# A Strassen layer kernel: loads and rotations in written order, the rotary table by another queue, S4 in S2's place, and another order at the start

## The chip, the cores and the metric

The kernel runs on one core of one Trainium2 chip. The metric is device time in microseconds (us) of one execution; three executions of the kernel before took 1544.78, 1542.77 and 1547.8, median 1544.78. The engines are TensorE (PE, with its weight loads PEld), VectorE (DVE), ScalarE (ACT), GpSimd (POOL) and SyncE (SP, which here only issues DMAs). ACT and POOL issue DMAs too.

## What is computed

One encoder layer for 1024 tokens of width 2048, in float32:

```python
def hybrid_layer(x, w_in, w_out, norm_w, decay_fwd, decay_bwd, gn_w, gn_b, sink):
    h = rms_norm(x, norm_w)
    proj = h @ w_in
    ...
    rq, rk, rv, rg, aq, ak, av, ag = jnp.split(proj, splits, axis=-1)
    y_ret = retention_branch(rq, rk, rv, decay_fwd, decay_bwd, gn_w, gn_b) * jax.nn.silu(rg.astype(jnp.float32))
    y_att = window_attention_branch(aq, ak, av, sink) * jax.nn.silu(ag.astype(jnp.float32))
    y = jnp.concatenate([y_ret, y_att], axis=-1).astype(x.dtype)
    return x + y @ w_out
```

proj has 6656 columns: eight retention heads of 128 (q, k, v and gate), and window attention with eight query heads and two key/value heads. The q and k of both are turned by rotary tables; the retention's covers all 128 columns of a head. A group norm with gn_w and gn_b follows the retention. A final RMSNorm follows the layer.

## The kernel before

**Products.** Both projections are done by Strassen's scheme in Winograd's form: a matrix product of 2 x 2 blocks in seven products, with sums of blocks ahead and behind. For the input projection the inner dimension is cut in two parts, the columns in blocks of 512. A *unit* is one part of one block: its weights are the four quarters a11, a12, a21, a22 (128 x 1024 each, 512 KB), and there are 26 units, in four phases (PHASES). The seven products come in the order 1, 2, 6, 5, 7, 3, 4 and take as weights, in this order, a11, a12, S2 = a22 - S1 (tile s2), S3 = a21 + a22 (kept in a21), S1 = a11 - a21 (kept in a11), S4 = a12 - S2 (kept in a12) and a22. The trace calls all quarters "a" and s2 "s". The x side of the products lies in the tiles c.

Each operand is split for float32 precision: wH is the value rounded by ACT (L87), wL what is left, by DVE (L84). A step is three matmuls of 128 x 512 (mm3): wH by the high part of c (L98), wH by its low part (L99), wL by the high part (L100); a product has 24 matmuls. wH and wL have two buffers, so that operands are made about a product ahead of PE. The results leave PSUM by ACT copies and DVE additions into tiles ct (L259, L91), and from there to DRAM as pr (on SP for the first part, on POOL with addition for the second).

**What sets the order.** PE's, SP's and POOL's instructions stand in the order of the program. advance(), called every six matmuls (a *tick*), lets the running jobs take a step each: attention, retention, gating, loads; idle(n) in a job skips n ticks. ACT's and DVE's instructions are put in written order up to tick 33; from there a scheduler chooses their order. operands() writes the operands of a unit; then(n, k) issues the next unit's quarter on SP at the point where the tile comes free.

**The start.** PE warms up on the identity (L1001), turns vec (norm_w, gn_w and gn_b, 32 rows) to columns (L1008), and transposes x's first four row tiles (xt, L1015). ACT rounds the transposed banks into c (L896), DVE makes the low part (L897, from_bank), and the value itself is kept in src (L902 on ACT, L904 on DVE: keep_bank). The squares of x (L362 on ACT, L364 on DVE) give the RMS factors; the rows of tiles 4 to 7 are scaled by them (scale_x, L377) before their transposes (L383).

**Attention and retention.** rotate() turns the attention's q and k (its products are L482). The softmax of window attention is L560 to L575; it reads the tiles snk and bnd. The retention's heads are fed by next_of(), which loads a head's q or k (tile qT or kT, L689) and its halves swapped (rx, L695) from pr, and multiplies them by the table rot (1 MB, loaded at L863) on DVE (L702, L704). Its decay factors come from decays(). sd are the score tiles of a head.

**The end.** gating() loads mix and pr on ACT's queue, out_operands() and project() run the output projection in four more units, and finish() (from L1308) writes the rows scaled by the final norm's weight fw.

## Time and profile before

| quantity | value |
|---|---|
| median of three executions | 1544.78 us (1542.77 to 1547.8) |
| the profiled execution | 1540.42 us |
| its span, first to last instruction | 1538.6 us |
| mean granted clock of PE | 0.996 |
| PE busy, share of the span | 1515.1 us, 98% |
| DVE busy | 1085.5 us, 71% |
| ACT busy | 688.4 us, 45% |
| POOL busy | 150.8 us, 10% |
| HBM traffic over the span | 204 GB/s |

A row of the timeline has the start in us, the time in us, the engine (SPq is SP's DMA issue), the line of the kernel, the operation, what it writes and reads, and in brackets the idle time of the engine before it with what ended it. A busy share is an average over stages with different limits, so the table by stretches of time is to be read beside it: the busy time of each engine in a stretch, in us, with the number of its instructions.

### The profile page before, as it was taken

What the parts mean: (1) busy time and instruction counts of PE and PEld (TensorE: products, weight loads), DVE (VectorE), ACT (ScalarE), POOL (GpSimd) and SP (SyncE); (2) the same over time, 40 slices, a digit from 0 to 9 for tenths busy, and PEclk for the clock granted to TensorE, in tenths of its full rate; (3) what the DMA queues carried; (4) which work ended last, traced back from release to release, by engine and by line L of the source; (5) the groups of instructions that cost most, each with busy time, mean ns of one, the idle gap of its engine ahead of it and who ended that gap; (6) DMA issues with size and microseconds to landing.
All of it is one profiled execution on the core that took longest, in us unless ns stands there. A gap on an engine that the chain in (4) does not pass through costs nothing.

```text
span 1538.6 us, 20487 instructions
## 1 busy us (share of the span) xinstructions
PE 1515.1 (98%) x7413; PEld 1274.3 (83%) x7413; DVE 1085.5 (71%) x1941; ACT 688.4 (45%) x1147; POOL 150.8 (10%) x168
## 2 busy tenths in 40 slices
PE   8999999999999999998999999999999999999997
PEld 7788888788888888887888888888888888888886
DVE  6885595557757585745877787779756966776766
ACT  6643463234535453533354434444444643543425
POOL 0000001111010000001211100001121102020001
PEclk9999999999999999999999999999999999999999
DMA  8268656899664415787577556469789688394756
GB/s 301 83 219 295 249 189 169 214 229 243 162 193 136 147 61 176 248 285 181 138 184 212 151 192 216 154 236 339 192 251 241 145 278 166 82 205 161 220 178 249
DMA packets 150533, 306.59 MB, mean 199 GB/s; under 512 B 13440, under 2 KB 71200, under 8 KB 141472
## 3 DMA queue, kind: packets, MB, share of 16 engines
q1 hardware_dynamic: 125744, 251.78, 48.0%
q0 software_dynamic: 19584, 35.66, 15.4%
q10 hardware_dynamic: 5104, 17.84, 3.2%
q8 instruction: 58, 0.95, 0.2%
q14 instruction: 43, 0.35, 0.1%
HBM read 190.68 MB, written 122.95 MB: 204 GB/s over the span
## 4 chain that ended last, share of the span: by engine, by line
PE 85%; DMA 6%; DVE 5%; ACT 1%; issue 1%; SPq 1%; POOL 0%; POOLq 0%; DVEq 0%; ACTq 0%
PE pj L100 21%; PE pj L98 21%; PE pj L99 21%; PE ax L99 5%; PE ax L100 5%; PE ax L98 5%; PE ax L771 2%; PE ax L498 1%; DVE wL L84 1%; DMA a<-in_w_in_dram 1%; PE ax L575 1%; DVE c L84 1%; DMA kept<-c 1%; PE ax L818 1%; PE ax L738 1%
## 5 line engine op out<-in xcount | busy, mean ns | idle before, releaser
L98 PE MATMUL pj<-c,wH 128*128 128x512 f32 x1448 | 579.4, 400 | 1.7 <-ACT wH L87 1.7
L100 PE MATMUL pj<-c,wL 128*128 128x512 f32 x1448 | 567.2, 392 | 4.3 <-DVE wL L84 4.1
L99 PE MATMUL pj<-c,wH 128*128 128x512 f32 x1448 | 565.9, 391 | 2.2 <-DVE c L897 1.1
L84 DVE TENSOR_TENSOR wL<-a,wH 128x1024 fp32r<-128x1024 f32 (+1 forms) x185 | 224.8, 1215 | 180.3 <-ACT wH L87 177.6
L100 PEld LDWEIGHTS pj<-c,wL 128*128 128x128 f32 x1448 | 272.3, 188 | 65.2 <-DVE wL L84 7.0
L87 ACT CAST wH<-a 128x1024 fp32r<-128x1024 f32 (+1 forms) x185 | 193.8, 1047 | 282.8 <-PE pj L99 119.6
L99 PEld LDWEIGHTS pj<-c,wH 128*128 128x128 f32 x1448 | 272.9, 188 | 53.7 <-DVE c L84 2.2
L98 PEld LDWEIGHTS pj<-c,wH 128*128 128x128 f32 x1448 | 272.9, 188 | 52.4 <-ACT wH L87 2.2
L259 ACT COPY ct<-pj 128x512 f32<-128x512 f32 x200 | 115.8, 584 | 214.3 <-PE pj L100 213.6
L249 POOL DMA_DIRECT2D pr<-ct x104 | 92.0, 955 | 836.8 <-DVE ct L91 725.0
L91 DVE TENSOR_TENSOR ct<-pj,ct 128x512 f32<-128x512 f32 x170 | 113.6, 687 | 81.2 <-PE pj L100 80.6
L99 PE MATMUL pj<-wL,c 128*128 128x512 f32 x224 | 87.3, 390 | 0.0
L98 PE MATMUL pj<-wH,c 128*128 128x512 f32 x224 | 87.2, 389 | 0.0
L100 PE MATMUL pj<-wH,c 128*128 128x512 f32 x224 | 87.1, 389 | 0.0
L99 PE MATMUL ax<-wL,c 128*128 128x512 f32 x208 | 81.0, 390 | 0.0
L98 PE MATMUL ax<-wH,c 128*128 128x512 f32 x208 | 80.9, 389 | 0.0
L100 PE MATMUL ax<-wH,c 128*128 128x512 f32 x208 | 80.9, 389 | 0.0
L84 DVE TENSOR_TENSOR wL<-s,wH 128x1024 fp32r<-128x1024 f32 x31 | 37.8, 1221 | 27.0 <-ACT wH L87 27.0
L99 PEld LDWEIGHTS pj<-wL,c 128*128 128x128 f32 x224 | 42.0, 188 | 9.1 <-DVE wL L84 0.3
L87 ACT CAST sH<-st 128x128 fp32r<-128x128 f32 x112 | 30.1, 297 | 43.5 <-DVE st L785 29.4
L98 PEld LDWEIGHTS pj<-wH,c 128*128 128x128 f32 x224 | 42.0, 188 | 8.8
L100 PEld LDWEIGHTS pj<-wH,c 128*128 128x128 f32 x224 | 42.0, 188 | 8.6
(222 smaller groups left out, 2023.6 us busy)
## 6 DMA issues: line engine op xcount, KB each, us to landing
a<-in_w_in_dram SPq DMA_DIRECT2D x103, 512.0 KB, 4.8
kept<-c SPq DMA_DIRECT2D x28, 1024.0 KB, 7.6
c<-kept SPq DMA_DIRECT2D x28, 1024.0 KB, 8.9
pr<-ct SPq DMA_DIRECT2D x104, 256.0 KB, 4.9
pr<-ct POOLq DMA_DIRECT2D x104, 256.0 KB, 6.0
a<-in_w_out_dram SPq DMA_DIRECT2D x18, 512.0 KB, 4.7
rx<-pr SPq DMA_DIRECT2D x64, 128.0 KB, 4.9
ysrc<-mix ACTq DMA_DIRECT2D x16, 512.0 KB, 4.9
```

The source lines that it names most:

```text
L84: nc.vector.tensor_tensor(out=dst, in0=src, in1=high.bitcast(F32), op=ALU.subtract)
L87: nc.scalar.copy(out=dst_h, in_=src)
L91: nc.vector.tensor_tensor(out=dst, in0=a, in1=b, op=ALU.add)
L98: nc.tensor.matmul(po, aH, bH, start=first, stop=False, **kw)
L99: nc.tensor.matmul(po, aH, bL, start=False, stop=False, **kw)
L100: nc.tensor.matmul(po, aL, bH, start=False, stop=last, **kw)
L249: nc.gpsimd.dma_start(out=dst, in_=t, accum_op=ALU.add)
L259: nc.scalar.copy(out=t, in_=bank)
L498: nc.tensor.transpose(pt[:, blk(t)], src[:, blk(b * 4 + t)], ident)
L575: nc.tensor.transpose(pt[:, blk(j)], s[:, blk(j)], ident)
L738: nc.tensor.matmul(sc[:, blk(t)], kT[:, c], qT[:, c], start=True, stop=True)
L771: nc.tensor.matmul(p, k_tok[:, c], vd[:, c, d], start=True, stop=True)
```

## The change

The change has several parts that lie at different places of the program.

- **Written order.** behind() keeps an instruction behind all that was written ahead of it for its engine, where the scheduler had a choice. It is used for S1 = a11 - a21 from tick 33 on, for rotate()'s products, for the rotation of the retention's head 0, and for gating's loads.
- **S4 in S2's place.** S4 is written to s2 instead of a12. a12 comes free with its own product's operand, and the next unit's a12 is issued right behind its a11.
- **rot** is issued by POOL at the start of heads() instead of by SP; q's loads of head 0 come four ticks earlier, their swapped halves go to tiles of the tag sd, and the rotation waits four ticks more.
- **The start.** vec is norm_w alone and is issued first on ACT's queue; its transpose stands behind those of x's tile 0. gn_w and gn_b are loaded in decays() and transposed there.
- **x's squares and scaling** come in another order: from_bank is cut into rounded (ACT) and left_over (DVE), and for odd k ACT's second reading of the bank stands ahead of DVE's. x's tiles 6 and 7 are scaled one and two ticks earlier, tile 5 one later, and tile 7 on ACT.
- gating waits six ticks instead of four between loads, and the factor sqrt(D) on fw is taken into the squares (scale D**-0.5) and the constants of the last norm.

```diff
     def sub(dst, a, b):
-        nc.vector.tensor_tensor(out=dst, in0=a, in1=b, op=ALU.subtract)
+        return nc.vector.tensor_tensor(out=dst, in0=a, in1=b, op=ALU.subtract)
...
+    def behind(it, ins):
+
+        if it:
+            tc.keep_in_program_order(ins)
...
             yield operand(a11)
-            yield operand(a12)
+            op = operand(a12)
             s2 = wp.tile([P, M, 2 * P], F32, name="s2", tag="s2")
-            sub(a11, a11, a21)
+            behind(clock[0] >= 33, sub(a11, a11, a21))
             sub(s2, a22, a11)
+            yield op
             yield operand(s2)
             add(a21, a21, a22)
             op = operand(a21)
             then(2, 1)
             yield op
             op = operand(a11)
+            sub(s2, a12, s2)
             then(1, 1)
+            if u + 1 < len(units):
+                then(1, 2)
             yield op
-            sub(a12, a12, s2)
-            op = operand(a12)
-            then(1, 2)
+            op = operand(s2)
+            if u + 1 == len(units):
+                then(1, 2)
             yield op
...
     def scale_x(t):
 
-        nc.vector.tensor_scalar(out=xh[t, 0], in0=xh[t, 0], scalar1=rms[:, t:t + 1], scalar2=None, op0=ALU.mult)
+        if t == NT - 1:
+            nc.scalar.activation(out=xh[t, 0], in_=xh[t, 0], func=AF.Copy, scale=rms[:, t:t + 1])
+        else:
+            nc.vector.tensor_scalar(out=xh[t, 0], in0=xh[t, 0], scalar1=rms[:, t:t + 1], scalar2=None, op0=ALU.mult)
...
-    vec = st.tile([KT + 2 * RH, P], F32, name="vec")
+    vec = st.tile([KT, P], F32, name="vec")
...
-    load_x(nc.sync, 0)
-    load_x(nc.scalar, 1)
...
+    load_x(nc.sync, 0)
+    nc.scalar.dma_start(out=vec, in_=norm_w[0].rearrange("(k p) -> k p", p=P))
     half_of_a11(0)
-    for r0, n, of in ((0, KT, norm_w), (KT, RH, gn_w), (KT + RH, RH, gn_b)):
-        nc.scalar.dma_start(out=vec[r0:r0 + n, :], in_=of[0].rearrange("(k p) -> k p", p=P))
+    load_x(nc.scalar, 1)
...
                 for t, f in zip(ts, cs):
-                    nc.vector.tensor_tensor(out=t[u], in0=t[u], in1=f[u], op=ALU.mult)
+                    behind(True, nc.vector.tensor_tensor(out=t[u], in0=t[u], in1=f[u], op=ALU.mult))
...
-        passing = wp.tile([P, 4 * H2 + 5], F32, name="passing", tag="ct", bufs=8)
+        passing = wp.tile([P, 4 * H2 + 5 + P], F32, name="passing", tag="ct", bufs=8)
...
+        for r0, of in ((0, gn_w), (RH, gn_b)):
+            nc.sync.dma_start(out=gn[r0:r0 + RH], in_=of[0].rearrange("(k p) -> k p", p=P))
...
         yield from idle(8)
+        pt = ax()
+        nc.tensor.transpose(pt[:, 0:H2], gn, ident[0:H2, 0:H2])
+        nc.scalar.copy(out=vec_t[:, KT:], in_=pt[:, 0:H2])
...
-                    beside.append(ret.tile([P, HALF], F32, name="rx", bufs=2))
+                    beside.append(ret.tile([P, HALF], F32, name="rx", tag="sd" if h == 0 and c == T_RQ else "rx", bufs=2))
...
-                yield from idle(7)
+                yield from idle(7 if h or c == T_RK else 11)
                 for i in range(2):
                     u, b = t[:, half(i)], beside[i]
-                    nc.vector.tensor_tensor(out=u, in0=u, in1=rot[:, 0, half(i)], op=ALU.mult)
+                    behind(h == 0, nc.vector.tensor_tensor(out=u, in0=u, in1=rot[:, 0, half(i)], op=ALU.mult))
...
             def heads():
+                nc.gpsimd.dma_start(out=rot, in_=rot_r)
                 while to_load:
                     yield
                 yield from idle(3)
-                nc.sync.dma_start(out=rot, in_=rot_r)
                 yield
                 start(next_of("kT", T_RK, 0))
-                yield from idle(7)
+                yield from idle(3)
                 start(next_of("qT", T_RQ, 0))
...
-            from_bank(1, k, pt)
-            keep_bank(1, k, pt)
+            for read in (rounded, keep_bank, left_over) if k % 2 else (rounded, left_over, keep_bank):
+                read(1, k, pt)
             squares(k, 0, k % 2 == 0, 1)
...
     def sums_of_x():
-        at = {5: (4, 4), 7: (5, 5), 9: (6, 6), 11: (7, 7), 14: (0, 1), 16: (2, 3)}
-        ready = {8: (4, 6), 12: (6, 8), 17: (0, 4)}
-        scaled = {9: 4, 10: 5, 13: 6, 14: 7}
+        ready = {8: (4, 6), 11: (6, 8), 17: (0, 4)}
+        both = {5: 4, 7: 5, 8: 6, 10: 7}
+        second = {13: 0, 14: 1, 15: 2, 16: 3}
+        scaled = {9: (4,), 11: (5,), 12: (6, 7)}
...
-    pv = pj()
-    nc.tensor.transpose(pv[:, 0:KT + 2 * RH], vec, ident[0:KT + 2 * RH, 0:KT + 2 * RH])
-    nc.scalar.copy(out=vec_t, in_=pv[:, 0:KT + 2 * RH])
-    nc.vector.tensor_scalar(out=nw, in0=nw, scalar1=D ** 0.5, scalar2=None, op0=ALU.mult)
     for t in range(4):
-        if t < 2:
-            squares(t, 0, t == 0, 0)
         for k in range(M):
             nc.tensor.transpose(pts[k][:, blk(t)], xh[t, 0][:, blk(k)], ident)
+        if t == 0:
+            squares(t, 0, True, 0)
+            pv = pj()
+            nc.tensor.transpose(pv[:, 0:KT], vec, ident[0:KT, 0:KT])
+            nc.scalar.copy(out=vec_t[:, 0:KT], in_=pv[:, 0:KT])
+            nc.vector.tensor_scalar(out=nw, in0=nw, scalar1=D ** 0.5, scalar2=None, op0=ALU.mult)
...
-                        yield from idle(4 if part == 0 else 5)
+                        yield from idle(6 if part == 0 else 5)
...
-        yield from idle(6)
-        nc.scalar.mul(fw, fw, D ** 0.5)
```

Where the instructions stand, at three places. First PE at the start of the program, before:

```order
L1001 MATMUL pj<-ident 128x128 x8
L1008 MATMUL pj<-ident,vec 128x32
L1015 MATMUL ax<-ident,xt 128x128 x4
L1001 MATMUL pj<-ident 128x128 x2
L1015 MATMUL ax<-ident,xt 128x128 x4
```

and with the change:

```order
L1018 MATMUL pj<-ident 128x128 x8
L1026 MATMUL ax<-ident,xt 128x128 x4
L1030 MATMUL pj<-ident,vec 128x16
L1018 MATMUL pj<-ident 128x128 x2
L1026 MATMUL ax<-ident,xt 128x128 x4
```

The transpose of vec has 16 columns instead of 32 and has moved behind the four transposes of x's first tile.

Second, DVE in the unit whose S2 is formed at 449 us, beside attention (a_3634 is a12, a_3683 a22, a_3577 a11 and then S1, a_3493 a21; qbL belongs to attention), before:

```order
L84 TENSOR_TENSOR wL<-a_3577,wH 128x1024
L94 TENSOR_TENSOR a_3577<-a_3577,a_3493 128x1024
L84 TENSOR_TENSOR wL<-a_3634,wH 128x1024
L84 TENSOR_TENSOR qbL<-q,qbH 128x256
L94 TENSOR_TENSOR s_3814<-a_3683,a_3577 128x1024
L84 TENSOR_TENSOR qbL<-q,qbH 128x256
L91 TENSOR_TENSOR a_3493<-a_3493,a_3683 128x1024
L94 TENSOR_TENSOR a_3634<-a_3634,s_3814 128x1024
L560 ISA s,nm<-ax,bnd,snk 128x256
L560 ISA nm 128x1
L560 ISA s,nm<-ax,bnd,snk 128x256
```

and with the change (a_3581 is a11, a_3583 a12, a_3686 a22, a_3496 a21):

```order
L84 TENSOR_TENSOR wL<-a_3581,wH 128x1024
L84 TENSOR_TENSOR qbL<-q,qbH 128x256 x2
L84 TENSOR_TENSOR wL<-a_3583,wH 128x1024
L94 TENSOR_TENSOR a_3581<-a_3581,a_3496 128x1024
L94 TENSOR_TENSOR s_3758<-a_3686,a_3581 128x1024
L91 TENSOR_TENSOR a_3496<-a_3496,a_3686 128x1024
L571 ISA s,nm<-ax,bnd,snk 128x256
L571 ISA nm 128x1
L571 ISA s,nm<-ax,bnd,snk 128x256
L571 ISA nm 128x1
L574 COPY s<-snk 128x1
L84 TENSOR_TENSOR wL<-s_3758,wH 128x1024
```

Both qbL have moved ahead of a12's low part, S1 has moved behind it, and S4 (before, the subtraction from a_3634) no longer stands between S2 and attention's softmax (ISA).

Third, DVE in the unit that is worked from about 692 us, beside the rotation of the retention's head 0 (a_6117 is a11 and then S1, a_6154 a12, a_6195 a22, a_6071 a21 and then S3), before:

```order
L84 TENSOR_TENSOR wL<-a_6117,wH 128x1024
L94 TENSOR_TENSOR a_6117<-a_6117,a_6071 128x1024
L702 TENSOR_TENSOR kT<-kT,rot 128x512 x2
L704 TENSOR_TENSOR rx<-rx,rot 128x512
L84 TENSOR_TENSOR wL<-a_6154,wH 128x1024
L91 TENSOR_TENSOR kT<-kT,rx 128x512
L704 TENSOR_TENSOR rx<-rx,rot 128x512
L91 TENSOR_TENSOR kT<-kT,rx 128x512
L94 TENSOR_TENSOR s_6316<-a_6195,a_6117 128x1024
L702 TENSOR_TENSOR qT<-qT,rot 128x512 x2
L91 TENSOR_TENSOR a_6071<-a_6071,a_6195 128x1024
L84 TENSOR_TENSOR wL<-s_6316,wH 128x1024
```

and with the change (a_6122 is a11, a_6124 a12, a_6198 a22, a_6074 a21):

```order
L84 TENSOR_TENSOR wL<-a_6122,wH 128x1024
L718 TENSOR_TENSOR kT<-kT,rot 128x512
L720 TENSOR_TENSOR rx<-rx,rot 128x512
L91 TENSOR_TENSOR kT<-kT,rx 128x512
L718 TENSOR_TENSOR kT<-kT,rot 128x512
L84 TENSOR_TENSOR wL<-a_6124,wH 128x1024
L94 TENSOR_TENSOR a_6122<-a_6122,a_6074 128x1024
L94 TENSOR_TENSOR s_6287<-a_6198,a_6122 128x1024
L720 TENSOR_TENSOR rx<-rx,rot 128x512
L91 TENSOR_TENSOR a_6074<-a_6074,a_6198 128x1024
L91 TENSOR_TENSOR kT<-kT,rx 128x512
L84 TENSOR_TENSOR wL<-s_6287,wH 128x1024
```

S1 has moved behind the first half of k's rotation and a12's low part, and q's rotation (qT), which stood between S2 and the low part of S2, has moved behind both.

The same place on SP, before:

```order
L1036 DMA c_5824<-kept_3_138 128x2048
L165 DMA a_6117<-in_w_in_dram 128x4x256
L1036 DMA c_5936<-kept_4_139 128x2048 x2
L165 DMA a_6154<-in_w_in_dram 128x4x256
L863 DMA rot<-in_rot_r_dram 128x2048
L689 DMA kT<-pr_73 128x1024
L695 DMA rx<-pr_73 64x512 x4
L165 DMA a_6195<-in_w_in_dram 128x4x256
L689 DMA qT<-pr_65 128x1024
L695 DMA rx<-pr_65 64x512 x4
```

and with the change:

```order
L696 DMA db<-in_dist_b_dram 128x128
L1056 DMA c_5827<-kept_3_138 128x2048
L170 DMA a_6122<-in_w_in_dram 128x4x256
L170 DMA a_6124<-in_w_in_dram 128x4x256
L1056 DMA c_5939<-kept_4_139 128x2048 x2
L705 DMA kT<-pr_73 128x1024
L711 DMA rx<-pr_73 64x512 x4
L170 DMA a_6198<-in_w_in_dram 128x4x256
L705 DMA qT<-pr_65 128x1024
L711 DMA rx<-pr_65 64x512 x4
```

a12's load (the third row before) has moved next to a11's, and rot is gone from SP. On POOL it stands between the last store of pr_68 and the first of pr_81, which is the store that POOL issued at 670.52 us before.

More of the change, by code (lines that the diff above doesn't have):

```diff
@@ L1286, in summed @@
         if whole and tt == NT - 1:
[L1287 removed]
+            nc.vector.tensor_tensor_reduce(out=junk, in0=r, in1=r, scale=1.0 / D, scalar=part[tt], op0=ALU.mult, op1=ALU.add, accum_out=rs)
         else:
[L1289 removed]
+            nc.scalar.activation(out=junk, in_=r, func=AF.Square, scale=D ** -0.5, accum_out=ssq[:, tt, c:c + 1])
         if whole:
```

46 lines of the change are left out of this document (23 added, 23 removed).

## The prediction

> **What bounds the kernel now.** I read the share of busy time first, then the table by stretch, then what TensorE waited for.
>
> ```profile
> span 1538.6 us, 20487 instructions
> PE 1515.1 (98%) x7413; PEld 1274.3 (83%) x7413; DVE 1085.5 (71%) x1941; ACT 688.4 (45%) x1147; POOL 150.8 (10%) x168
> ...
> 0.00:40.00 40.00, 35.05 (x175) 28.41 (x176) 25.42 (x45) 24.98 (x45) 2.12 (x8) 1.00 0.79 289
> 40.00:80.00 40.00, 38.11 (x175) 30.03 (x174) 36.41 (x46) 25.32 (x35) 1.01 (x1) 1.00 0.23 80
> 80.00:660.00 580.00, 577.85 (x2838) 488.90 (x2837) 385.74 (x733) 259.64 (x475) 35.39 (x40) 1.00 0.65 199
> 660.00:720.00 60.00, 55.38 (x247) 45.50 (x246) 29.82 (x38) 15.79 (x23) 8.78 (x10) 0.94 0.79 236
> 720.00:1528.00 808.00, 808.00 (x3983) 681.18 (x3982) 604.44 (x1073) 360.34 (x568) 102.55 (x108) 1.00 0.69 198
> ```
>
> After a stretch's length come the busy times of TensorE (PE), its weight loads, DVE, ACT and POOL, then PE's granted clock, the DMA share and GB/s. PE is busy for all 808 us from 720 to 1528 us; the change issues no fewer matmuls, so nothing can be won there. Its idle time elsewhere is 4.95 us before 40, 1.89 to 80, 2.15 to 660 and 4.62 to 720: 13.6 us together. A little more is hidden where the matmuls run at a lower clock (0.94 in the fourth row). **The gain is bounded by about 13.6 + 2 us**, 1% of the span, and the change has to be read stall by stall. Two of its waits by cause (us in total, times, longest), which the parts below take up; the others stand there at their places:
>
> ```profile
> PE pj L100 <- DVE wL L84: 4.1, 4, 2.9
> ...
> PE pj L99 <- DVE c L897: 1.1, 2, 0.8
> ```
>
> **Part 1, the first 80 us.**
>
> ```profile
> DMA to landing us min/median/max: 3.8/4.4/4.7
> ...
> 1.37 3.48 PE L1001 MATMUL pj<-ident 128*128 128x128 f32 x16 [1.37 <-POOL ident masks.py:199]
> 6.50 0.21 PE L1008 MATMUL pj<-ident,vec 32*128 32x32 f32 x1 [1.65 <-DMA vec<-in_gn_b_dram]
> ...
> 6.64 0.66 PE L1015 MATMUL ax<-ident,xt 128*128 128x128 f32 x4
> ...
> 9.35 0.60 PE L1015 MATMUL ax<-ident,xt 128*128 128x128 f32 x4
> ...
> 10.40 0.50 PE L98 MATMUL pj<-c,wH 128*128 128x512 f32 x1
> ...
> 24.01 0.69 ACT L902 ACTIVATE src<-ax,vec_t 128x512 f32<-128x512 f32 x1 [1.36 <-DVE c L897]
> 24.60 1.05 ACT L362 ACTIVATE junk<-xt 128x1024 bf16<-128x1024 f32 x1
> ...
> 24.03 0.50 PE L99 MATMUL pj<-c,wH 128*128 128x512 f32 x1 [0.83 <-DVE c L897]
> ...
> 35.59 0.33 PE L383 MATMUL ax<-ident,xt 128*128 128x128 f32 x1 [0.39 <-DVE xt L377]
> 36.26 0.33 PE L383 MATMUL ax<-ident,xt 128*128 128x128 f32 x1 [0.34 <-DVE xt L377]
> ```
>
> The first row is the landing time of x's first four loads. PE stands still until 6.50 for the third piece of vec (gn_b), and only then transposes x, tile by tile, the last at 9.35: three steps, (9.35 - 6.64) / 3 = 0.90 us each. With norm_w alone, first on ACT's queue, and x0's transposes ahead of vec's, PE goes on when its opening matmuls end (1.37 + 3.48 = 4.85); x0 still leaves first on SP, in the first us, and 4.4 us later, near 5.0, it is there. x1 leaves as ACT's second instead of its first and x3 as its third instead of its fifth: near 5.6 and 6.1, both before their turn. The last transposes then start near 5.0 + 3 x 0.90 = 7.7: 1.7 us earlier. That holds for the first L98 if the two evictions ahead of it, which had no other wait, follow; the lower bound is 0, if the weights, which come no earlier, hold the first products back.
>
> The 24.03 stall: L99 waits for DVE's c, because ACT's scaled copy waited 1.36 us for DVE's reading of the same bank, and DVE then waited for the next rounded part from ACT. For odd k the change lets ACT read twice, then DVE. That stall's 0.83 us of idle, with its lengthened first matmul about 1.1, should go: +1.1. The two waits at 35.59 and 36.26 (0.73) should go with the earlier scaling of x6 and x7, one of which moves to ACT; but an ACT activation of this size takes 1.05 us (24.60), more than the two scalings on DVE lie apart (36.26 - 35.59), and stands ahead of the chain of copies. I give it +0.2 (bounds -0.5 and +0.7). From 40 to 80 us DVE is busy 36.41 of 40 us, so the shift passes through but nothing is added. **Head: 1.7 + 1.1 + 0.2 = 3.0 us**, bounds 0 and 3.7.
>
> **Part 2, S4 in S2's place, and the pinned subtraction.**
>
> ```profile
> 449.22 1.23 DVE L94 TENSOR_TENSOR s<-a,a 128x1024 f32<-128x1024 f32 x1 [2.75 <-DMA a<-in_w_in_dram]
> 450.36 0.42 DVE L84 TENSOR_TENSOR qbL<-q,qbH 128x256 fp32r<-128x256 f32 x1
> 450.70 1.22 DVE L91 TENSOR_TENSOR a<-a,a 128x1024 f32<-128x1024 f32 x1
> 451.83 1.22 DVE L94 TENSOR_TENSOR a<-a,s 128x1024 f32<-128x1024 f32 x1
> ...
> 455.67 0.68 PE L575 MATMUL ax<-ident,s 128*128 128x128 f32 x4 [0.94 <-DVE s L567]
> ...
> 281.33 0.68 DVE L482 TENSOR_TENSOR rx<-rx,rt 64x512 f32<-64x512 f32 x1 [6.58 <-DMA rx<-pr]
> ```
>
> No DVE instruction is added per unit. At 449, DVE waited 2.75 us for a22 and then worked through its queue; PE's wait at 455.67 is the end of it (0.94 idle, 1.1 with the slower next matmul). In the new order of that place qbL (450.70 - 450.36 = 0.34) stands ahead of the wait, and the subtraction for S4 (as long as 451.83 - 450.70 = 1.13) behind the softmax: the softmax starts 1.5 us earlier and the stall goes, even if a22 lands no earlier: **+1.1** (bounds 0 and 1.2). Of PE's four waits for wL (4.1 us), 2.9 is the one at 713.50 below and 0.8 follows the DVE wait of 6.58 us at 281.33. There the new order has the same rows in the same sequence: nothing. Of the remaining 0.4, most is at 212, where the last product's wL stood behind other work and its operand is now ready earlier: **+0.3** (bounds 0 and 0.4). Unit 1's third operand now has four rows ahead of it that were behind it; and every later unit of the input projection gets a new order. I take **-0.5** for small new stalls (bounds 0 and -2), as PE found none from 720 on with nearly the same work.
>
> **Part 3, the retention's first loads, 660 to 720 us.**
>
> ```profile
> 660.00:670.00 10.00, 10.00 (x55) 8.60 (x54) 2.47 (x4) 3.33 (x7) 0.00 (x0) 1.00 0.27 113
> ...
> 700.00:710.00 10.00, 8.26 (x37) 6.51 (x37) 5.96 (x9) 1.80 (x3) 0.86 (x1) 1.00 1.09 286
> 710.00:720.00 10.00, 7.12 (x25) 5.53 (x26) 9.32 (x12) 1.37 (x2) 1.77 (x2) 0.66 0.33 49
> ...
> L563 DVE COPY s<-snk x64: 131/148/154, 271.0 to 655.6; 128x1 f32<-128x1 f32 x64
> ...
> 670.52 1.77 POOL L249 DMA_DIRECT2D pr<-ct  x2 [224.75 <-DVE ct L91]
> ...
> 685.64 0.50 SPq L863 DMA_DIRECT2D rot<-in_rot_r_dram  x1
> ...
> 703.35 2.41 SPq L695 DMA_DIRECT2D rx<-pr  x4
> ...
> 707.45 1.23 DVE L94 TENSOR_TENSOR s<-a,a 128x1024 f32<-128x1024 f32 x1 [2.81 <-DMA a<-in_w_in_dram]
> 709.88 1.29 DVE L702 TENSOR_TENSOR qT<-qT,rot 128x512 f32<-128x512 f32 x2 [1.20 <-DMA qT<-pr]
> ...
> 707.76 0.39 PE L100 MATMUL pj<-c,wL 128*128 128x512 f32 x1
> 709.89 0.50 PE L98 MATMUL pj<-c,wH 128*128 128x512 f32 x1 [1.74 <-ACT wH L87]
> ...
> 713.50 0.80 PE L100 MATMUL pj<-c,wL 128*128 128x512 f32 x1 [2.88 <-DVE wL L84]
> 714.09 0.63 PE L98 MATMUL pj<-c,wH 128*128 128x512 f32 x1
> ...
> 717.51 0.52 PE L100 MATMUL pj<-c,wL 128*128 128x512 f32 x1
> ```
>
> DMA is full from 700 to 710 (1.09). a22 lands at 707.4; sub s, its cast and its wL follow, and between sub s and wL DVE waits another 1.20 for qT. PE's steps are 0.228 us elsewhere (24 matmuls, a product, take 5.5 us). Here it starts L98 at 709.89 instead of 707.76 + 0.23 = 707.99, 1.90 late. The wait of 2.88 before 713.50 costs about 3.0 start to start. The next step takes 0.59, and then eight come (717.51 - 714.09) / 8 = 0.43 apart: 0.4 + 8 x 0.2 = 2.0. In all **about 6.9 us**, the largest term.
>
> The 1 MB of rot moves from SP's queue, ahead of a22, to POOL's, which is idle for 224.75 us before 670.52; its only waits are for tiles whose last reader is attention's softmax, 655.6. From 660 to 670 the DMA engines are 27% busy, so rot fits there. At 286 GB/s, the rate from 700 to 710, 1.05 MB less ahead of it brings a22 forward by 3.6 us; I take 3.4, to 704.0. With qT's rotation no longer between sub s and wL, DVE needs for sub s, half a product of rx, the sum for a21, kT's sum and wL s 1.13 each for the three of 1024 columns and half of that, 0.6, for the two of 512: 4.6 us, so wL ends at 708.6. PE, unstalled, reaches that L100 at 707.99 + 0.46 = 708.45. So 0.2 us remain, and I leave 0.5 for q's loads: **+6.2**, bounds 2.5 (a22 not earlier, only the wait for qT and part of the low clock gone) and 6.9.
>
> The Trainium skill ("TensorE: Matmul & The Clock Gate", "HAM oscillation") says that idle gaps above about 3.4 us let the clock fall to half. Here the longest single gap was 2.88 us and the granted clock in that stretch still fell to 0.66. By the letter of the page those 2.0 us would not belong to the stall, and the part would bring 4.3; the trace has them right behind it, so the measurement decides.
>
> **Part 4, what costs nothing.** gn's loads and a 16-column transpose go into decays, near 180 us; the transpose of all 32 columns took 0.21 us, so about -0.2, inside the -0.5 above. The scaling of fw, the idle steps of gating and the changed constants lie in 720 to 1538, where PE has no wait; after its last matmul the same instructions remain: 0.
>
> **Sum.** 3.0 + 1.1 + 0.3 - 0.5 + 6.2 = 10.1 us. The profiled execution took 1540.42 (span 1538.6), so 1530.3. The median of the three runs stands 4.4 higher, at 1544.78; less 10.1 it is **1534.7**.
>
> **The rivals.** *Head 0's loads stay late* (0.18). The DMA engines are full at 700 to 710, and moving loads among queues adds no bandwidth; qT and its rx are now issued sooner and share the engines with a22. Then 710 gives 2.5 of its 6.9 us and the gain is 10.1 - 3.7 = 6.4, or 4.2 where q's loads come later too: 1540.5. This would also be the result if rot itself came late. The rows speak against it: POOL's two stores at 670.52 took 1.77 us, 0.9 each, so rot is out long before 670. The Trainium skill ("SBUF — State Buffer", "SBUF: two separate sides") warns of just this: GpSimd cannot write descriptors while a two-port DVE operation runs, 620 ns then becoming 3100 ns. Were an issue of 0.9 us stretched five times, an estimate from that page, rot would leave near 661 instead of 657; no run here shows it.
>
> *The head's gain is swallowed* (0.14): loads of weights or the chain of ACT copies and DVE subtractions set the time to 80 us. Gain 10.1 - 3.0 = 7.1: 1537.6.
>
> *Slower: q's pinned rotation stands in front of a21's wL* (0.05). DVE now runs, behind wL s, qT's product, rx's product, S4's subtraction, a sum, a product, two evictions, rx's product and then wL of a21: 0.6 + 0.6 + 1.13 + 0.6 + 0.6 + 1.2 + 0.6 + 1.13 = 6.5 us. PE wants that wL one product (5.5 us) after 708.45, at 713.9. So q's loads have to be there by 707.4. Each us later costs one, and the clock's 2.0 once. It is slower than before from 9 us late (9 + 2.0 = 6.9 + 3.9 of the other parts); if they land at 722, 14.6 us late, it is 16.6 - 10.8 = 5.8 slower: 1550.6. Against it: the stop of SP until 703.35, for kT's rx buffers, goes, since q's rx gets others.
>
> *It does not do what it says* (0.05): the scheduler's order elsewhere opens stalls as large as those closed: 1544.8.
>
> **How the numbers follow.** Forecast 0.58, at 1534.7. A measurement here tells about 0.3% (4.6 us) from no change. Faster: 0.58 + 0.14 + 0.08 of the late loads = 0.80; same: the other 0.10 + 0.05 = 0.15; slower 0.05. The range goes from 1530.5 (all stalls closed, about 14 us) to 1541.5 (late loads, with a little less at the head); it leaves out about 0.15.
>
> **What would show it.** The first L98 near 8.7 instead of 10.40; no DVE wait at 24.03; no PE row with a wait at 455; a22's subtraction at 704 and no PE gap over 0.5 us from 709 to 714, with a granted clock of 1.00 there; the wait at 281.33 unchanged. I am wrong if a22 still lands after 706, or if new waits for wL appear in units that had none.

## The result, and the profile after

The changed kernel took 1533.12 us (median of four, 1531.5 to 1533.56) against 1545.47 of the kernel before; the ratio is 0.9919 with a 95% interval of 0.9900 to 0.9937. That is 12.4 us less, where 10.1 were forecast; the time lies 1.6 us from the forecast of 1534.7, which was taken from the first median of 1544.78, and inside the range. The profiled executions, though, differ by 6.9 us only (1540.42 and 1533.51; spans 1538.6 and 1531.7). The page of after, and then its table by stretch, in the columns shown before:

```profile
span 1531.7 us, 20492 instructions
PE 1513.6 (99%) x7414; PEld 1273.8 (83%) x7414; DVE 1084.5 (71%) x1940; ACT 690.3 (45%) x1148; POOL 151.8 (10%) x169
```

```profile
0.00:40.00 40.00, 37.00 (x183) 30.19 (x184) 25.97 (x46) 28.27 (x50) 3.48 (x8) 1.00 0.78 289
40.00:80.00 40.00, 37.57 (x173) 29.97 (x172) 36.58 (x46) 23.84 (x32) 1.01 (x1) 1.00 0.23 79
80.00:660.00 580.00, 578.41 (x2839) 489.21 (x2839) 384.34 (x731) 260.69 (x476) 36.09 (x41) 1.00 0.65 200
660.00:720.00 60.00, 58.33 (x277) 48.56 (x276) 34.52 (x46) 18.65 (x28) 8.79 (x10) 1.00 0.85 248
```

PE's idle time before 40 us fell from 4.95 to 3.00, from 660 to 720 from 4.62 to 1.67, and the clock there is 1.00 instead of 0.94. From 40 to 80 it rose, from 1.89 to 2.43. To compare places I use one more measure, the *delay*: every start-to-start distance of two matmuls, less the 0.228 us (or what its kind takes elsewhere), summed over a stretch. It counts waits and matmuls at a lower clock alike.

| stretch | delay before, us | delay after, us | forecast gain, us |
|---|---|---|---|
| 0 to 80 | 10.6 | 9.5 | 3.0 |
| 80 to 680 | 2.8 | 2.5 | 1.1 + 0.3 - 0.5 |
| 680 to 720 | 7.0 | 1.8 | 6.2 |
| from 720 | -2.4 | -2.1 | 0 |

(Below zero: for some small matmuls there the measure allows a little too much.) The last 0.7 us lie behind the last matmul. Three places of after, from the timeline of PE, of DVE and of PE again:

```profile
4.94 0.87 PE L1026 MATMUL ax<-ident,xt 128*128 128x128 f32 x4
...
7.11 0.66 PE L1026 MATMUL ax<-ident,xt 128*128 128x128 f32 x4 [0.49 <-DMA xt<-in_x_dram]
...
10.20 0.50 PE L98 MATMUL pj<-c,wH 128*128 128x512 f32 x1
...
701.47 1.23 DVE L94 TENSOR_TENSOR s<-a,a 128x1024 f32<-128x1024 f32 x1
...
704.95 1.22 DVE L84 TENSOR_TENSOR wL<-s,wH 128x1024 fp32r<-128x1024 f32 x1
...
692.33 0.50 PE L99 MATMUL pj<-c,wH 128*128 128x512 f32 x1 [1.67 <-DMA c<-kept]
```

x0 is transposed at 4.94, as forecast, but x1 only at 7.11, and the first L98 comes at 10.20 instead of 8.7. At 701.47 DVE forms S2 with no wait, and its low part ends at 706.2, earlier than the 708.6 of the forecast; 1.4 us of this is the lead with which the whole program comes there (the store of pr that SP issued at 654.34 stands at 652.95). A wait that was not forecast stands at 692.33. What the two profiles do not show is where the other 5.5 us of the medians come from.

### The profile page after: what moved, and what is told of

Read it like the earlier page. It is cut to its first block, busy times and chain, and to the rows that moved or that the text cites. A ratio compares the mean times of both kernels' runs of the same rounds, so it can differ in the third digit from the quotient of the medians.

```text
span 1531.7 us, 20492 instructions
## 1 busy us (share of the span) xinstructions
PE 1513.6 (99%) x7414; PEld 1273.8 (83%) x7414; DVE 1084.5 (71%) x1940; ACT 690.3 (45%) x1148; POOL 151.8 (10%) x169
## 4 chain that ended last, share of the span: by engine, by line
PE 78%; issue 13%; DVE 3%; DMA 3%; ACT 1%; POOL 1%; SPq 0%; POOLq 0%; ACTq 0%; DVEq 0%
PE pj L100 19%; PE pj L99 19%; PE pj L98 19%; PE ax L99 5%; PE ax L100 5%; PE ax L98 5%; PE ax L787 2%; PE ax L509 1%; PE ax L586 1%; DMA xt<-in_x_dram 1%; PE ax L754 1%; PE ax L834 1%; DMA c<-kept 1%; DVE c L84 1%; DMA pr<-ct 1%
## 5 line engine op out<-in xcount | busy, mean ns | idle before, releaser
L98 PE MATMUL pj<-c,wH 128*128 128x512 f32 x1448 | 578.6, 400 | 0.3 <-DVE ct L91 0.3
L98 PEld LDWEIGHTS pj<-c,wH 128*128 128x128 f32 x1448 | 272.3, 188 | 50.4 <-ACT ct L268 0.6
L87 ACT CAST wH<-a 128x1024 fp32r<-128x1024 f32 (+1 forms) x160 | 167.6, 1048 | 248.0 <-PE pj L99 144.9
L84 DVE TENSOR_TENSOR wL<-a,wH 128x1024 fp32r<-128x1024 f32 (+1 forms) x160 | 194.7, 1217 | 112.2 <-ACT wH L87 108.8
L84 DVE TENSOR_TENSOR wL<-s,wH 128x1024 fp32r<-128x1024 f32 x56 | 68.5, 1223 | 91.7 <-ACT wH L87 91.6
L98 PE MATMUL pj<-wH,c 128*128 128x512 f32 x224 | 87.1, 389 | 0.0
L98 PE MATMUL ax<-wH,c 128*128 128x512 f32 x208 | 80.9, 389 | 0.0
L87 ACT CAST wH<-s 128x1024 fp32r<-128x1024 f32 x56 | 59.1, 1056 | 16.4 <-PE ax L100 8.8
L98 PEld LDWEIGHTS pj<-wH,c 128*128 128x128 f32 x224 | 42.0, 188 | 8.8
## 6 DMA issues: line engine op xcount, KB each, us to landing
c<-kept SPq DMA_DIRECT2D x28, 1024.0 KB, 10.1
```

What stands on the lines that cost most here:

```text
L84: nc.vector.tensor_tensor(out=dst, in0=src, in1=high.bitcast(F32), op=ALU.subtract)
L87: nc.scalar.copy(out=dst_h, in_=src)
L98: nc.tensor.matmul(po, aH, bH, start=first, stop=False, **kw)
```

## The experiments

**1. The kernel before once more.** No edit.

> The kernel before, unchanged, profiled once more. The medians differ by 12.4 us, but the two profiled executions' spans by 6.9 (1538.6 and 1531.7), and the four times of before spread over 5.0 us, those of after over 2.1. Theory: the stall near 710 us depends on when a full DMA delivers a22 and on the clock behind it, and is longer in most executions than in the profiled one. Then this profile has the same waits of TensorE as the first everywhere but from 690 to 730 us, where the sum of its delays is 6.9 us or more (up to 12), and its span is longer by what stands there. Rival: the difference is spread thinly over the run (a lower granted clock, or longer waits at the start); then 690 to 730 stays at 6.9 within 0.5 us in an execution that is slower than 1540.

1545.75 us (median of twelve; 1541.2 to 1549.9); the profiled execution took 1549.35, 8.9 more than the first one of the same kernel. Its timeline, PE at the start, PE near 1160 us, then DVE ahead of that; below it DVE and PE near 1010 us, and its stretch from 720:

```profile
6.82 0.28 PE L1008 MATMUL pj<-ident,vec 32*128 32x32 f32 x1 [1.67 <-DMA vec<-in_gn_b_dram]
7.03 1.12 PE L1015 MATMUL ax<-ident,xt 128*128 128x128 f32 x4
...
12.62 0.50 PE L98 MATMUL pj<-c,wH 128*128 128x512 f32 x1
...
1159.95 0.50 PE L100 MATMUL pj<-c,wL 128*128 128x512 f32 x1 [1.76 <-DVE wL L84]
...
1161.26 0.63 PE L99 MATMUL pj<-c,wH 128*128 128x512 f32 x1
...
1155.27 1.23 DVE L94 TENSOR_TENSOR s<-a,a 128x1024 f32<-128x1024 f32 x1 [4.15 <-DMA a<-in_w_in_dram]
...
1157.55 1.22 DVE L1198 TENSOR_TENSOR ysrc<-ysrc,yt 128x1024 f32<-128x1024 f32 x1
1158.68 1.22 DVE L84 TENSOR_TENSOR wL<-a,wH 128x1024 fp32r<-128x1024 f32 x1
```

```profile
1008.30 1.22 DVE L84 TENSOR_TENSOR wL<-a,wH 128x1024 fp32r<-128x1024 f32 x1
1009.43 0.48 DVE L84 TENSOR_TENSOR sL<-st,sH 128x128 fp32r<-128x128 f32 x2
...
1009.97 0.33 PE L99 MATMUL ax<-sL,qhl 128*128 128x128 f32 x1 [1.43 <-DVE sL L84]
```

```profile
720.00:1520.00 800.00, 796.69 (x3921) 670.84 (x3920) 593.36 (x1048) 349.16 (x549) 100.95 (x102) 1.00 0.68 193
```

Both theories fall. The delay from 690 to 730 was 5.6 us here, less than the 7.0 of the first profile. The rest stands at single places that had no wait in the first profile: 3.3 us of idle time after 720, at 1010 and 1160 us, and a start that is 2.2 us later. At 1155 DVE waits for a22 as at 710, for 4.15 us; but here a12's low part, which lacks nothing, stands behind the wait, while at 710 it stood ahead. a22 landed 11.6 us after its issue, 7.2 in the first profile, among gating's loads. The wait at 1010 is of another kind: DVE has no idle time there, and PE waits for sL, the low part of the retention's state, which stands behind a weight's low part.

**2. The three main parts, each alone on the kernel before.** The start: the edits to vec, gn, from_bank, sums_of_x and scale_x. The second part: operands() and rotate(). The third: rot, q's loads, sd and the rotation of head 0.

> Before, with only the edits to the first 80 us (norm_w alone and first, gn in decays, x's squares and scaling in another order). Theory: the first matmul of 128x512 starts near 10.2 us instead of 10.40, since x's tiles land later (7.1, 8.2, 8.6 instead of 4.9, 6.4, 7.1); the wait at 24.03 is gone, the two at 35.59 and 36.26 become one; the sum of delays before 80 us falls by 1.2 us (from 10.6 to 9.4), and the stall at 710 is as before. Time 1 to 2 us below before: 1543 to 1545. Rival: what 6.9 against 12.4 us leaves open lies at the start, where the DMA's order differs from execution to execution; then 3 us or more below before.

> Before, with only S4 in S2's place, S1 in written order, a12's load next to a11's, and rotate's products in written order. Theory: the wait at 455 us (1.1) goes; the stall at 710 stays with 4 us or more, since rot is still ahead of a22; and TensorE waits 1 to 2 us near 692 to 700 for c loaded from kept, because a12's 512 KB now pass two kept loads. Net 0 to -3: 1542 to 1546. Rival: this part takes the stall at 710 away; then 1535 to 1539.

> Before, with only the edits to the retention's first loads (rot by GpSimd's queue, q's loads earlier, q's swapped halves in tiles of the tag sd, rotation of head 0 in written order). Theory: a22's lateness behind rot was the cause of the 6.9 us at 710; without rot in SP's queue it is gone, and there is no wait for c loaded from kept at 692, since a12's load stays behind the kept loads: delays from 690 to 730 below 1 us, the rest of the waits as before. Time 1545 less 6 to 10: 1535 to 1539. Rival: the order of DVE and the place of a12's load (the other part) did it; then 3 us or more of delay remain here.

| kernel | median, us | ratio to before (95%) |
|---|---|---|
| start alone | 1541.90 | 0.9974 (0.9954 to 0.9994) |
| second part alone | 1538.55 | 0.9948 (0.9926 to 0.9970) |
| third part alone | 1541.11 | 0.9983 (0.9958 to 1.0008) |

Before had 1544.24 in these rounds; the three gains (2.3, 5.7, 3.1) add up to 11.1 of the 12.4, but the interval of the third reaches past 1, so that its gain is not clear of noise. What is left of the change, gating's loads and the final norm, was not run alone. None of the three times lies where its theory had it (1543 to 1545, 1542 to 1546, 1535 to 1539); the second part's lies where its rival had it. The second part is the largest, where 0.9 had been forecast for it. Its DVE at the place of the stall at 1160, and its stretch from 720:

```profile
1145.07 1.23 DVE L84 TENSOR_TENSOR wL<-a,wH 128x1024 fp32r<-128x1024 f32 x1 [2.46 <-DMA a<-in_w_in_dram]
1146.21 1.22 DVE L94 TENSOR_TENSOR a<-a,a 128x1024 f32<-128x1024 f32 x1
1151.16 1.23 DVE L94 TENSOR_TENSOR s<-a,a 128x1024 f32<-128x1024 f32 x1 [3.73 <-DMA a<-in_w_in_dram]
1152.31 1.22 DVE L91 TENSOR_TENSOR a<-a,a 128x1024 f32<-128x1024 f32 x1
1153.52 1.23 DVE L84 TENSOR_TENSOR wL<-s,wH 128x1024 fp32r<-128x1024 f32 x1
```

```profile
720.00:1521.00 801.00, 799.95 (x3939) 673.63 (x3938) 597.39 (x1065) 357.01 (x560) 100.75 (x105) 1.00 0.69 197
```

DVE waits as long as ever (3.73), yet a12's low part is done ahead of the wait, and S4 no longer stands between S2 and its low part: PE has no wait there. The waits at 455 and 1010 are gone too. With the whole change DVE does not even wait for a22 at this place in any of the seven profiles of after and its variants; of the seven others two have no wait there (before and the third part alone) and five one of 3.7 to 8.7 us. DVE in after, then the stretch from 1130 to 1150 in before, with the second part alone, and in after:

```profile
1144.20 1.23 DVE L94 TENSOR_TENSOR s<-a,a 128x1024 f32<-128x1024 f32 x1
```

```profile
1130.00:1150.00 20.00, 20.00 (x90) 16.57 (x89) 12.26 (x13) 9.75 (x11) 4.94 (x6) 1.00 1.06 346
...
1130.00:1150.00 20.00, 20.00 (x90) 16.57 (x89) 9.82 (x10) 8.81 (x10) 5.27 (x6) 1.00 1.07 336
...
1130.00:1150.00 20.00, 20.00 (x90) 16.56 (x89) 14.17 (x15) 10.25 (x12) 5.26 (x6) 1.00 0.91 217
```

The DMA engines are full in the first two rows (shares of 1.06 and 1.07) and not in the third (0.91), where ACT issues gating's loads in pairs about 11 us apart, while in before one comes every 0.4 to 6 us. gating's edits, which the forecast put at 0, may thus have a share in the gain; no run shows how much.

The delay from 690 to 730 fell to 2.5 us with the second part alone (0.6 for c from kept, 1.9 for S2's low part) although rot stayed on SP, and to 1.4 with the third part alone, although a12 stayed in its place (one wait for a12's low part is left, at 708.63): each removes most of that stall in the one profile taken of it, and their gains there do not add. DVE near 710 in before, then with the second part alone:

```profile
701.50 1.22 DVE L84 TENSOR_TENSOR wL<-a,wH 128x1024 fp32r<-128x1024 f32 x1
...
712.23 1.22 DVE L84 TENSOR_TENSOR wL<-s,wH 128x1024 fp32r<-128x1024 f32 x1
```

```profile
706.38 1.23 DVE L94 TENSOR_TENSOR s<-a,a 128x1024 f32<-128x1024 f32 x1 [0.69 <-DMA a<-in_w_in_dram]
...
710.17 1.22 DVE L84 TENSOR_TENSOR wL<-s,wH 128x1024 fp32r<-128x1024 f32 x1
```

a12's low part (701.50) was ahead of S2 (707.45) in before already. What the second part changed here is that a22 landed 1.1 us sooner and that the sum for a21 moved behind S2's low part, which came 2.1 us sooner; PE then waited once, 1.70 us, instead of 1.74 and 2.88, and the clock did not fall. With the start alone the stall stayed, at 8.6 us; there the first L98 came at 9.56.

**3. The two halves of the second part.** S1 pinned (kept in written order by behind()), with a12's operand written ahead of it:

```diff
-            yield operand(a12)
+            op = operand(a12)
...
-            sub(a11, a11, a21)
+            behind(clock[0] >= 33, sub(a11, a11, a21))
             sub(s2, a22, a11)
+            yield op
```

> Before, with S1 = a11 - a21 written with a12's operand and kept behind it in DVE's order; S4 stays in a12's place and the loads stay where they were. The part of both together took 5.7 us off, and in two more profiles without it TensorE waited at 1007 to 1010 (1.4 to 1.6 us) and at 1158 to 1160 us (3.1 and 1.9 us, then about 1.4 at a lower clock), waits that the first profile of before did not have. Theory: those waits, and most of that at 710, come from DVE waiting for a22 with a12's low part queued behind the wait; the pin puts a12's low part ahead, so this alone gives 4 to 6 us (1538.5 to 1540.5), the waits at 1159 and 710 fall below 2 us each, and no wait for c from kept stands near 692. Rival: it is a12's earlier load and S4's place; then less than 2 us here, and the wait at 1159 in the profile as long as it was.

and S4 in S2's place, with a12's load early:

```diff
+            sub(s2, a12, s2)
             then(1, 1)
+            if u + 1 < len(units):
+                then(1, 2)
             yield op
-            sub(a12, a12, s2)
-            op = operand(a12)
-            then(1, 2)
+            op = operand(s2)
```

> Before, with S4 written to S2's tile and a12's load next to a11's; S1's subtraction is not pinned and stands where it was written. Theory (the pin does it): 0 to 2 us below before (1542.5 to 1544.5); DVE still waits for a22 ahead of a12's low part in at least some units, and TensorE's waits at 710 or at 1159 stay above 2 us in sum. Rival (S4's place does it): 4 to 6 us below before, 1538.5 to 1540.5.

The pin alone: 1543.93 us, ratio 0.9988 (0.9970 to 1.0005). S4 alone: 1548.58, ratio 1.0018 (0.9999 to 1.0038); before had 1543.46 in these rounds. The pin gives less than 2 us, as the rival had it, but S4's place does not give the rest either, and came out slower than the 1542.5 to 1544.5 expected of it; only the two together, with rotate's pin, give 5.7. DVE and PE of the pinned kernel, then of the one with S4:

```profile
1153.33 1.23 DVE L84 TENSOR_TENSOR wL<-a,wH 128x1024 fp32r<-128x1024 f32 x1 [2.46 <-ACT wH L87]
...
1159.65 1.23 DVE L94 TENSOR_TENSOR s<-a,a 128x1024 f32<-128x1024 f32 x1 [3.96 <-DMA a<-in_w_in_dram]
1160.79 1.22 DVE L91 TENSOR_TENSOR a<-a,a 128x1024 f32<-128x1024 f32 x1
1161.93 1.22 DVE L94 TENSOR_TENSOR a<-a,s 128x1024 f32<-128x1024 f32 x1
1163.06 1.22 DVE L84 TENSOR_TENSOR wL<-s,wH 128x1024 fp32r<-128x1024 f32 x1
```

```profile
1155.95 1.23 DVE L94 TENSOR_TENSOR s<-a,a 128x1024 f32<-128x1024 f32 x1 [8.74 <-DMA a<-in_w_in_dram]
...
1159.36 1.22 DVE L84 TENSOR_TENSOR wL<-a,wH 128x1024 fp32r<-128x1024 f32 x1
...
1160.63 0.80 PE L100 MATMUL pj<-c,wL 128*128 128x512 f32 x1 [6.35 <-DVE wL L84]
```

With the pin, a12's low part is ahead of the wait, but S4's subtraction (1161.93) still stands ahead of S2's low part, and PE lost 1.4 us at 1164. With S4's place alone that row is gone, but a12's low part waits behind a22: PE waits 6.35 us for it. In these two profiles one half only moves the wait at 1160 to the next row in the queue. The stall at 710 stayed with either half (6.6 and 5.9 us of delay from 690 to 720); the pin could not help there, as a12's low part stood ahead already. How much of the 5.7 us rotate's pin has, which was in neither kernel, was not tried.

**4. Two mends of after.** The late x at the start, and the wait at 692 for a tile c that is loaded from kept, where parts of the x side lie in DRAM. First the small loads of before once more, then a12's load in its old place:

```diff
     load_x(nc.scalar, 1)
+    spare = st.tile([2 * RH, P], F32, name="spare")
+    for r0, of in ((0, gn_w), (RH, gn_b)):
+        nc.scalar.dma_start(out=spare[r0:r0 + RH], in_=of[0].rearrange("(k p) -> k p", p=P))
```

> After, with two loads of 4 KB (gn_w and gn_b into a tile that nothing reads) put between x1 and x3 on ACT's queue, as they stood before. In after x's tiles landed at 4.4, 7.1, 8.2 and 8.6 us, in before at 4.6, 4.9, 6.4 and 7.1, and SP issued the second half of a11 and the next 1 MB of x at 2.15 and 2.63 instead of 4.95 and 5.38. Theory: only eight loads can be on their way before an issue waits for an earlier one to land (the ninth issue waits in both), and the two small loads had kept those 1.25 MB back; with them x lands earlier again, the last transposes start near 7.7 to 8.3 instead of 9.15, the first matmul of 128x512 near 8.7 to 9.3 instead of 10.20: 1 us less than after, 1532. Rival: x's landing differs from execution to execution by itself (the first L99 came at 11.2 and 13.4 in two profiles of before, 10.35 with the start's edits alone); then the issue times return to those of before but x lands no earlier than in after.

```diff
             then(1, 1)
-            if u + 1 < len(units):
-                then(1, 2)
             yield op
             op = operand(s2)
-            if u + 1 == len(units):
-                then(1, 2)
+            then(1, 2)
             yield op
```

> After, with a12's load where it was in the program before (behind S4's operand), and all else as in after. Theory: in after TensorE waited 1.67 us at 692 for c loaded from kept, since a12's 512 KB had passed two kept loads in SP's queue (at about 300 GB/s worth 1.7 us); here the kept loads leave first and that wait is gone, while a12 still lands before its operand is wanted near 700. 1531 to 1532.5 against 1533.1 of after (ratio to before 0.9905 to 0.9915 against 0.9919). Rival: the wait at 692 comes from DMA being full at that time whatever the order; then it stays above 1 us, or the same wait turns up for a12 near 699 to 703.

The medians were 1531.84 (ratio 0.9908, 0.9883 to 0.9932) and 1532.68 (0.9910, 0.9884 to 0.9937). The landing of x's loads in after, the same with the two small loads, and then SP's queue and PE with them:

```profile
DMA to landing us min/median/max: 3.7/6.2/6.9
```

```profile
DMA to landing us min/median/max: 4.6/4.6/4.9
```

```profile
3.45 0.38 SPq L452 DMA_DIRECT2D a<-in_w_in_dram  x1
4.40 0.38 SPq L363 DMA_DIRECT2D xt<-in_x_dram  x1
...
8.43 0.60 PE L1029 MATMUL ax<-ident,xt 128*128 128x128 f32 x4
...
9.48 0.50 PE L98 MATMUL pj<-c,wH 128*128 128x512 f32 x1
```

Two loads that nothing reads hold back the 1.25 MB behind them by 1.3 and 1.8 us, and x lands sooner after its issue. That holds in every profile of the new start: x1, x2 and x3 each landed earlier in the three with the small loads (between 5.6 and 7.3 us) than in any of the five without (between 6.0 and 8.6). In this pair it is worth 0.7 us (9.48 against 10.20), less than a measurement can tell, and it does not always reach the first L98: that came at 9.48, 10.07 and 9.46 in the three, at 9.56 to 10.30 in the five. With a12's load back, the delay from 690 to 720 was 0.5 us. Then both mends, both with rotate()'s products three ticks later, and after once more, on one chip:

> After, unchanged, to compare the next three with on one chip, and to see which of its waits return. From four times of 1531.5 to 1533.6: 1533, and no wait of TensorE above 1.2 us from 80 us on but the one for c from kept near 692 (1.8 in the first profile, between 0 and 2 here); none at 1007 to 1010 and none at 1158 to 1165, where three profiles without both halves of the second part had 1.4 to 6.5.

> After, with the two loads of 4 KB between x1 and x3, and a12's load back behind S4's operand. In single profiles the first brought the first matmul of 128x512 from 10.20 to 9.48 and the second took the wait at 692 from 1.83 to nothing; they lie 680 us apart. Theory: they add, 0.7 and up to 1.8: 1.5 to 2.5 us below after_again. Rival: the wait at 692 differs from execution to execution by itself (0.46 in the run with the small loads alone); then 0.5 to 1.2 below.

> As both_mends, and rotate() lets eight ticks pass between its loads and its products instead of five. DVE waited 6.58 us in before and 3.52 in after at 281 us for a product of rotate() whose operand landed at 281.4, with an eviction and a low part behind it in its order; TensorE lost 1.0 to 1.6 us there in nearly every profile. Theory: three ticks (4.1 us) later the operand has landed; the waits of TensorE at 282.6 and 284.3 are gone: 1 to 1.5 us below both_mends. Rival: the later step of attention runs into the next one and brings a wait of the same size between 284 and 460: same as both_mends.

After took 1530.99 us (ratio 0.9909, 0.9883 to 0.9934), both mends 1531.78 (0.9913), with the later products 1531.86 (0.9910): no gain, where 1.5 to 2.5 us had been expected of both mends and 1 to 1.5 of the later products. In this profile of after (span 1528.0) PE did not wait at 692 at all, and its first L98 came at 9.95: the waits that the mends remove are not in every execution. And one of the mends may have brought a wait of its own, here from both mends:

```profile
946.13 0.33 PE L99 MATMUL ax<-sL,qhl 128*128 128x128 f32 x1 [1.12 <-DVE sL L84]
```

All three profiles with a12's load back have such a wait for sL from 946 to 948, a delay of 1.0 to 1.4 us, and none of the five that have the second part with a12's early load; why was not followed up. The later products stayed at the same row of DVE's order, with a wait of 3.80 us; that run does not test what it was meant to test.

**5. rot by SP, all else as after.**

```diff
             def heads():
-                nc.gpsimd.dma_start(out=rot, in_=rot_r)
                 while to_load:
                     yield
                 yield from idle(3)
+                nc.sync.dma_start(out=rot, in_=rot_r)
```

> After, with rot issued by SP again, three ticks into heads() as before; all else of after stays (a12's low part ahead of the wait for a22, q's loads early). Theory: rot's 1 MB is ahead of a22 again and costs it 3 to 3.5 us of 300 GB/s, so a22 lands at 704 to 705 instead of 701.0; DVE then ends S2's low part about 708.5 to 709.5, where TensorE wants it at 708 or so: waits of 1 to 2.5 us between 700 and 715, as in the run with the second part alone (0.6 and 1.9): 1 to 3 us above after_again. Rival: with the new order of DVE the place of rot no longer matters: within 0.5 us of after_again, and no wait above 0.5 us there.

1533.92 us, 2.9 above after in the same rounds (each median of six, 1529.8 to 1533.3 for after and 1533.4 to 1534.5 here). a22 landed at 703.5, S2 was formed at 703.72, and PE waited again:

```profile
703.72 1.23 DVE L94 TENSOR_TENSOR s<-a,a 128x1024 f32<-128x1024 f32 x1
...
707.20 1.22 DVE L84 TENSOR_TENSOR wL<-s,wH 128x1024 fp32r<-128x1024 f32 x1
```

The delays were 1.2 us at 690.9 and 0.9 at 708.5. The theory holds: rot ahead of a22 costs 2 to 3 us even in the new order. The place of rot works in two ways, which were not measured apart: its 1 MB shares the DMA engines, and it stands in the row of DMAs behind which a22 is issued. SP issued a22 at 687.86 here, 0.06 us behind the landing of the eighth DMA ahead of it, a load of kept; in before it was the same (690.72 and 690.66). In after, without rot in the row and with a12 ahead of the loads of kept, the eighth was a12, which had landed at 686.61, and a22 was issued at 687.20.

## Why the prediction was right, and where it was not

**The bound.** "Busy for all 808 us from 720 to 1528 us ... nothing can be won there" is the step that failed. It is true of the one execution that was profiled, which at 1540.42 was 4.4 us faster than the median. Five further profiles without both halves of the second part (before again, start alone, third part alone, pin alone, S4 alone) have 2.1 to 7.3 us of idle time of PE from 720 to 1520, most of it at 1005 to 1010, 1075 to 1080 or 1158 to 1164; the eight profiles with the second part have 0.0 to 1.3. The bound of 13.6 + 2 us was one execution's, and the forecast put 0 where five of the six profiles without the whole second part lose 2 us or more.

**Part 1, 3.0 us.** The mis-sized step is "x1 ... and x3 ... both before their turn". They were issued earlier, but landed later (x1 7.06, x3 8.56): eight DMAs are under way on SP's and ACT's queues before an issue waits for a landing (in before the ninth is issued at 4.95, x1 having landed at 4.94; in after at 3.48, vec having landed at 3.47). The small loads of gn were two of the eight, and without them SP issued the second half of a11 and 1 MB of x at 2.15 and 2.63 instead of 4.95 and 5.38, into the same DMA engines. The 1.7 us became 0.2. The stall at 24.03 shrank from a delay of 1.1 to one of 0.3, at 22.79, nearly as forecast; the two at 35.59 and 36.26, for which +0.2 was given, became two of the same size (0.6 and 0.5), at 36.42 and 37.15. (The upper bound of 3.7 for the head does not follow either: 1.7 + 1.1 + 0.7 is 3.5.) In the medians the start was worth 2.3 us, and the profiles show a reason that the forecast lacked: in three of six with the old start PE, after its wait for vec, ran the transposes at about half speed (1.06 instead of 0.60 for four) and its first L98 came at 12.4 to 13.4, in the other three at 10.4 to 10.6; in eight with the new one it came at 9.5 to 10.3.

**Part 2, 1.1 + 0.3 - 0.5.** The stall at 455 went as worked out. That at 212 shrank to 0.2. The new small stalls were about as large as feared: 0.7 at 77, where two of 0.3 and 0.4 went, and 0.9 more in sum at 271 to 284. DVE's wait at 281 stayed (3.52 instead of 6.58). But the part was put at 0.9 us and measured 5.7. The step that failed is that its gain was counted only where the first profile had a wait; what the part does is put a12's low part ahead of every wait for a22, and a22 is late at other places in other executions. This explains the waits at 1158 to 1164 (that at 455 goes with S4 out of the softmax's way, and at 710 S2 and its low part came sooner, experiment 2). It does not explain those at 1005 to 1010, where DVE does not wait for a22, nor those at 1075 to 1080, where DVE waited 1.53 us for a value from POOL: they are missing in all eight profiles with the second part, and why is not shown.

**Part 3, 6.2 us.** The stretch went from 6.9 to 1.8 (and to 0 in the second profile of after), and the wait at 710 itself to nothing, so the sum is about right, but not its split. rot's move was held to be the cure; the second part alone took 4.4 of the 6.9 us away, with rot still on SP, as S2's low part came 2.1 us sooner and the 2.0 us of the lower clock did not come. Moving rot is worth 2.9 us on top. The margin was larger than forecast: a22 landed at 701.0, 3 us ahead of the 704.0, 1.4 of them by the lead of the whole program. Nor is its landing 6.4 us sooner than in before a matter of bytes alone, as the forecast reckoned: a22 was also issued 3.5 us sooner (687.20 instead of 690.72; experiment 5). And one step was left out: a12's 512 KB now pass two loads of kept in SP's queue, for 1.8 us at 692 in one of two profiles of after, 0.5 to 1.2 in the three other kernels with the whole second part and a12's early load, and nothing in the three with the load back. (The 4.3 us that the forecast gives for the part without the lower clock is 6.2 - 2.0 = 4.2.) The warning that was weighed (the Trainium skill, "SBUF — State Buffer", "SBUF: two separate sides") had no bearing here: rot took POOL 0.58 us to issue, at 655.10, and landed 9.9 us later.

**Part 4, put at 0.** That gating's edits cost and bring nothing is not shown: the wait for a22 near 1150, which five of the seven profiles without them have, is in none of the seven with them (experiment 2).

**Rivals and signs.** Late loads, the pinned rotation of q and a scheduler's order that opens as much as it closes did not come; that the head's gain would be swallowed came true in the profile (1.2 of 3.0) and not in the medians. Of the signs of being wrong the late a22 did not come; new waits for wL came, but small: those at 77 and 271 lie in units that had one before, and one of 0.24 us at 1233.83 in a unit of the output projection that had none. That the total agrees is luck: errors of opposite sign met, 1.8 us too many for the start and 1 for 710 in the one profiled execution, and 5.5 too few for what that execution did not show.

## What to carry to other kernels

A profile is one execution; a place where a DMA lands just in time is idle in some executions and not in others, so look at the slack of each wait, not only at the waits that showed, and profile the kernel before twice. In an in-order queue, put what is ready ahead of what waits, and look at the next row too: here half of such an edit moved the wait, or made it longer. A DMA that is issued earlier can land later when it lets others go ahead with it.

## What was not expected of the hardware

PE's clock fell after short waits. In the second profile of before a single wait of 1.76 us (1159.95) was followed, 1.3 us later, by 3.4 us of matmuls 0.43 us apart instead of 0.23:

```profile
1156.00:1160.00 4.00, 2.24 (x11) 1.54 (x9) 3.97 (x5) 0.78 (x2) 0.00 (x0) 1.00 0.95 207
1160.00:1164.00 4.00, 4.00 (x12) 3.16 (x13) 3.52 (x3) 2.20 (x3) 0.00 (x0) 0.64 0.73 254
1164.00:1168.00 4.00, 4.00 (x18) 3.28 (x17) 1.61 (x3) 1.33 (x2) 0.69 (x2) 0.93 0.52 152
```

The wait of 1.67 us at 692 in after had no such end, nor had that of 1.7 at 711 with the second part alone. The Trainium skill ("TensorE: Matmul & The Clock Gate", "HAM oscillation") puts the limit at gaps of about 3.4 us; this trace shows a fall after a gap of half that, and the measurement decides. So a wait of 1.9 us start to start can cost 1.9 us or, with eight steps 0.2 us longer, 3.5, and which of the two it is differs from execution to execution.
